# A hybrid decoder layer in split fp32r: gaps of 64 or 32 bytes behind the rows of the transposed activations

## The chip, the cores and the metric

The kernel runs on one core of one Trainium2 chip. The metric is the device time of one execution in microseconds. Three executions of the kernel before took 1139.84, 1139.86 and 1139.87 us, median 1139.86 us.

## The reference, cut to what matters

One layer of a decoder trunk over 256 tokens of width 2048, float32 throughout. The parts that bear on this case are five matrix products and what stands between them:

```python
hn = rmsnorm(x, norm_mix_g)                       # x: 256 x 2048
p = hn @ w_in + b_in                              # 2048 x 6152: conv a/g, q, k, v, o, gates
u = silu(group_norm(causal_dwconv(a * sigmoid(g))))   # 31 taps, 1024 channels
hm = group_norm(mlstm(q, k, v, i, f)) * sigmoid(o)    # 4 heads of 256
x = x + concat([u, hm]) @ w_out                   # 2048 x 2048
up = rmsnorm(x, norm_ffn_g) @ w_up                # 2048 x 11264
h = silu(causal_dwconv(up[:, :5632])) * up[:, 5632:]  # 3 taps
x = x + h @ w_down                                # 5632 x 2048
return rmsnorm(x, norm_final_g)
```

## The kernel before, in words

**Split products.** Each float32 operand is held as two float32r parts, `hi` (the value rounded) and `lo` (value minus `hi`). A product is three matmuls into one PSUM bank: `hi*hi`, `hi*lo` and `lo*hi`. The transposed activations are split once and stay in SBUF: `xp` (16 rows of k, for each row 256 tokens of `hi` and then 256 of `lo`), later `x1p` of the same form in the same place, `mixh` and `mixl` (16 rows of 256), and `ah` and `al` (44 rows of 256, each a buffer of its own). A "row" here is one block of 128 values of k, which lie on the partitions; along a partition a row of `xp` has 2048 bytes and one of `ah` 1024.

**Slabs.** The weights stream through SBUF in slabs, mostly of two rows of k by 512 columns. For each slab SyncE issues the load into one of 5 `raw` buffers, ScalarE casts it into one of 4 `hi` buffers (line 214), VectorE, or GpSimd for some slabs, subtracts into one of 4 `lo` buffers (line 215), and TensorE multiplies. Splitting runs three slabs ahead (`AHEAD`). The order of the work is the order of the slabs list; all other work is hung on slab numbers by `after`.

**Which operand moves.** TensorE loads 128 x 128 weights and streams a moving operand past them; each matmul here has a weight load of its own.

- `ws` groups (lines 241 to 243: conv a/g, q, k): slab columns are loaded as weights, 256 tokens of `xp` stream.
- gate and up (`wp_group`, lines 267 and 268): slab columns are loaded; one row of `x1p`, 512 wide (`hi` and `lo` side by side), streams past the slab's `hi`, then its first 256 past the slab's `lo`.
- `xs` groups (lines 286 to 288: o 344 wide, v and w_out 512 wide, w_down 512 wide) and `down_narrow` (lines 839 to 841, 256 wide): the other way round; 128 tokens of the activations are loaded and the slab's columns stream.

**Where the buffers lie.** In a partition, as the built program places them, taken mod 512 bytes: `xp` and `x1p` begin at 192, `mixh` and `mixl` at 192, `ah` and `al` at 160, all `hi` and `lo` buffers at 160. Every row, every block of 128 columns and every buffer is a multiple of 512 bytes long, so these places hold for every row; the one exception is o, whose 344-wide second row of a slab begins 1376 bytes on, at 0 mod 512. "Lead" below is the place of a weight load minus that of the stream it is loaded beside, mod 512: -32 in `ws`, gate and up; 0 in down and `down_narrow`; +32 in v, w_out and the first rows of o; +192 in the second rows of o.

Of the kernel before, what the change touches and what calls it, by code (L numbers as in the profile page):

```python
# [9 lines left out]
F32 = mybir.dt.float32  # L10
F32R = mybir.dt.float32r
# [4 lines left out]
P = 128  # L16
T = 256
NT = T // P
D = 2048
NK = D // P  # L20
# [4 lines left out]
NF = DFF // P  # L25
# [16 lines left out]
def hybrid_layer_kernel(  # L42
# [11 lines left out]
    cst = ctx.enter_context(tc.tile_pool(name="cst", bufs=1))  # L54
# [7 lines left out]
    def mm_bank(name):  # L62
        return ps.tile([P, 512], F32, tag="mm", name=name, bufs=4)

    def cv_bank(k, name):
        return ps.tile([P, 512], F32, tag=f"cv{k}", name=name)

    def ax_bank(name):
        return ps.tile([P, 512], F32, tag="ax", name=name, bufs=2)
# [7 lines left out]
    def v2(t):  # L77
        return t.rearrange("p (a b) -> p a b", a=2)
# [88 lines left out]
    def after(delay, fn, cost=0.0):  # L167
        tasks[cur[0] + delay].append((fn, cost))
# [48 lines left out]
    def w_slab(wap, kt, nk, col, w, fn, on_pool):  # L217
        if col is None:
            src = wap(kt)
        else:  # L220
            src = wap[kt * P:(kt + nk) * P, col:col + w].rearrange("(k p) c -> p k c", p=P)
        slabs.append(dict(src=src, w=w, nk=nk, mm=fn, pool=on_pool))
# [54 lines left out]
    def xs_slab(wap, col, w, stat, kt, first, last, st, done, on_pool):  # L277
        def fn(hi, lo):
            if first:
                st["b"] = [cv_bank(0, "xs0"), cv_bank(1, "xs1")] if st.get("cv") else [mm_bank("xs0"), mm_bank("xs1")]  # L280
            sh, sl = stat()
            for k in range(2):
                for tt in range(NT):
                    o = st["b"][tt][:, :w]
                    ts_ = slice(tt * P, (tt + 1) * P)
                    pe.matmul(o, sh[:, kt + k, ts_], hi[:, k, :w], start=first and k == 0, stop=False)  # L286
                    pe.matmul(o, sh[:, kt + k, ts_], lo[:, k, :w], start=False, stop=False)  # L287
                    pe.matmul(o, sl[:, kt + k, ts_], hi[:, k, :w], start=False, stop=last and k == 1)  # L288
            if last:
                done(st["b"])  # L290
        w_slab(wap, kt, 2, col, w, fn, on_pool)

    def xs_group(wap, col, w, stat, nk, done, on_pool):
        st = {}
        for kt in range(0, nk, 2):
            xs_slab(wap, col, w, stat, kt, kt == 0, kt + 2 == nk, st, done, on_pool)


    xT = {}
# [318 lines left out]
    def done_out(n):  # L618
        def fn(banks):
            cs = slice(n * 512, (n + 1) * 512)  # L620
            st = {}

            def ev():
                if "h2" not in xT:
                    xT["p2"] = cst.tile([P, NK, 2, T], F32R, tag="xp", name="x1p")
                    xT["h2"], xT["l2"] = xT["p2"][:, :, 0, :], xT["p2"][:, :, 1, :]
                x1 = xres["t"]
                for tt in range(NT):
                    dve.tensor_add(x1[:, tt, cs], x1[:, tt, cs], banks[tt])

            def sq():
                for tt in range(NT):
                    act.activation(banks[tt], xres["t"][:, tt, cs], AF.Square, accum_out=ssq[:, tt, n:n + 1])

            def tr(half):
                def f():
                    b = ax_bank("x1T")
                    st[half] = b
                    for k in range(2):
                        kt = 4 * n + 2 * half + k  # L640
                        for tt in range(NT):
                            pe.transpose(b[:, k * T + tt * P:k * T + (tt + 1) * P], xres["t"][:, tt, kt * P:(kt + 1) * P], ident)
                    for k in range(2):
                        kt = 4 * n + 2 * half + k
                        act.activation(xT["h2"][:, kt, :], v2(b)[:, k, :], AF.Copy, scale=g_ffn[:, kt:kt + 1])
                    for k in range(2):
                        kt = 4 * n + 2 * half + k
                        dve.scalar_tensor_tensor(xT["l2"][:, kt, :], v2(b)[:, k, :], g_ffn[:, kt:kt + 1],
                                                 xT["h2"][:, kt, :].bitcast(F32), op0=ALU.mult, op1=ALU.subtract)
                return f  # L650
            after(1, ev, 1300)
            after(2, tr(0), 800)
            after(3, tr(1), 800)
            after(3, sq)
            if n == 3:
                after(4, rs_ffn)
        return fn

    ffn = {}
# [13 lines left out]
    def open_ffn():  # L673
        if "ah" in ffn:
            return
        inner.close()
        fp = ctx.enter_context(tc.tile_pool(name="ffn", bufs=1))
        ffn["pool"] = fp
        ffn["ah"] = fp.tile([P, NF, T], F32R, tag="ah", name="ah")
        ffn["al"] = fp.tile([P, NF, T], F32R, tag="al", name="al")  # L680
        ffn["gp"] = [fp.tile([P, 2, FK - 1 + T], F32, tag=f"gp{i}", name=f"gp{i}") for i in range(2)]
        for g in ffn["gp"]:
            pool.memset(g[:, :, 0:FK - 1], 0.0)
# [16 lines left out]
    def done_gate(j):  # L700
        def fn(banks):
            s = [None, None]

            def ev():
                open_ffn()
                copy_halves(banks)
# [72 lines left out]
        dve.tensor_mul(o, o, ffn["gf"][:, c0:c0 + w])  # L779

    def load_gf():
        gfb = cst.tile([P, NK, 2, T], F32, tag="xp", name="gfb")
        ffn["gf"] = gfb.rearrange("p a h b -> p (a h b)")[:, 0:D]
        act.dma_start(ffn["gf"], bass.AP(tensor=norm_final_g.tensor, offset=norm_final_g.offset, ap=[[0, P], [1, D]]))

    def done_down(n, c0, w):
        def fn(banks):
            def ev():
                if n == 0:
                    load_gf()  # L790
                for tt in range(NT):
                    add_down(banks[tt], tt, n, c0, w)

            def gmul():
                for tt in range(NT):
                    mul_gf(tt, c0, w)
            after(1, ev)
            after(3, gmul)
            if n == 3:
                after(3, pre_sum)  # L800
        return fn
# [67 lines left out]
    for b in range(3):  # L869
        xs_group(w_in, OFF_O + OW * b, OW, get_xT, NK, done_o(b), True)  # L870
# [6 lines left out]
    for hp in range(2):  # L877
        xs_group(w_in, OFF_V + 512 * hp, W, get_xT, NK, done_v(hp), True)
# [17 lines left out]
    for n in range(3):  # L896
        xs_group(w_down, 512 * n, W, lambda: (ffn["ah"], ffn["al"]), NF, done_down(n, 512 * n, W), False)
# [1 line left out]
    down_narrow(4, 1792, 256, 4, SPLIT_BUFS)  # L899


    xT["p"] = cst.tile([P, NK, 2, T], F32R, tag="xp", name="xp")
    xT["h"], xT["l"] = xT["p"][:, :, 0, :], xT["p"][:, :, 1, :]
    for c in range(NK // 2):
        sl = slice(c * T, (c + 1) * T)
        if c:
# [73 lines left out]
    for i in range(len(slabs)):  # L980
# [30 lines left out]
        while bg and credit > 0:  # L1011
            name = bg[0][0].__name__
# [40 lines left out]
```

## Time and profile before

| | |
|---|---|
| median of three executions | 1139.86 us |
| the profiled execution, its own time | 1139.86 us |
| its span in the trace | 1138.1 us |
| granted TensorE clock, mean over the span | 0.998 |
| PE busy, matmuls | 1125.4 us, 6756 |
| weight loads busy | 1007.7 us |
| VectorE, ScalarE, GpSimd busy | 746.4, 579.4, 131.3 us |
| DMA | 215.43 MB, 189 GB/s |

The busy time of PE counts each matmul from its start to a modelled end, and neighbours overlap. What a matmul costs in a stream is therefore read here from starts: the distance between the starts of two neighbours. In the timeline the columns are the start, the duration (both us), the engine, the line, the operation, out<-in, the array's part and the stream's shape.

### The profile page before, as it was taken

How to read it: one execution, taken by the hardware profiler on the slowest of the kernel's cores; microseconds unless marked ns; L12 is line 12 of the kernel's file. 1: busy time of each engine (PE TensorE's matmuls, PEld its weight loads, DVE VectorE, ACT ScalarE, POOL GpSimd, SP SyncE). 2: the span in 40 equal slices, each digit the busy share in tenths (PEclk: the TensorE clock that was granted, in tenths of full speed). 3: DMA queues.
4: the chain of work that ended last, by engine and by line, in shares of the span. 5: the costliest groups of instructions: out<-in, count | busy, mean ns of one | idle time of the engine just before them, and what ended most of it. 6: DMA issues, size and time to landing. Idle time of an engine off the chain costs nothing.

```text
span 1138.1 us, 17456 instructions
## 1 busy us (share of the span) xinstructions
PE 1125.4 (99%) x6756; PEld 1007.7 (89%) x6756; DVE 746.4 (66%) x1138; ACT 579.4 (51%) x824; POOL 131.3 (12%) x100
## 2 busy tenths in 40 slices
PE   8999999999999999999999999999999999999997
PEld 8999999998888888888888888888888888888997
DVE  5498999987656457667666666676576645454543
ACT  4744576754445455545555555455555434343432
POOL 0343554534300000000000000000000000000000
PEclk9999999999999999999999999999999999999999
DMA  8864565565655666666666666666666667656652
GB/s 269 250 187 123 183 220 169 178 195 168 204 193 171 189 184 182 191 192 194 184 190 192 183 196 188 193 190 188 188 184 193 195 197 228 196 190 196 192 186 76
DMA packets 128459, 215.43 MB, mean 189 GB/s; under 512 B 7456, under 2 KB 44920, under 8 KB 127864
## 3 DMA queue, kind: packets, MB, share of 16 engines
q1 hardware_dynamic: 126824, 209.99, 60.9%
q10 hardware_dynamic: 1552, 4.33, 1.0%
q8 instruction: 53, 0.87, 0.3%
q14 instruction: 30, 0.25, 0.1%
HBM read 212.19 MB, written 2.10 MB: 188 GB/s over the span
## 4 chain that ended last, share of the span: by engine, by line
PE 95%; DVE 3%; ACT 1%; issue 1%; POOL 0%; POOLq 0%; ACTq 0%
PE gate L267 14%; PE up L267 14%; PE xs L287 9%; PE xs L286 9%; PE xs L288 9%; PE up L268 7%; PE gate L268 7%; PE ws L243 5%; PE ws L241 5%; PE ws L242 5%; PE xs L841 2%; PE xs L840 2%; PE xs L839 2%; DVE conv L376 2%; DVE lo L215 1%
## 5 line engine op out<-in xcount | busy, mean ns | idle before, releaser
L215 DVE TENSOR_TENSOR lo<-raw,hi 128x1024 fp32r<-128x1024 f32 (+2 forms) x353 | 435.2, 1234 | 327.3 <-ACT hi L214 321.3
L214 ACT CAST hi<-raw 128x1024 fp32r<-128x1024 f32 (+2 forms) x400 | 411.7, 1032 | 452.8 <-PE xs L288 153.4
L267 PE MATMUL gate<-x1p,hi 128*128 128x512 f32 x704 | 245.0, 390 | 0.0
L267 PE MATMUL up<-x1p,hi 128*128 128x512 f32 x704 | 244.5, 390 | 0.0
L268 PE MATMUL up<-x1p,lo 128*128 128x256 f32 x704 | 198.5, 282 | 0.0
L268 PE MATMUL gate<-x1p,lo 128*128 128x256 f32 x704 | 198.5, 282 | 0.0
L267 PEld LDWEIGHTS up<-x1p,hi 128*128 128x128 f32 x704 | 132.2, 188 | 27.7
L267 PEld LDWEIGHTS gate<-x1p,hi 128*128 128x128 f32 x704 | 132.2, 188 | 27.6
L241 PE MATMUL ws<-xp,hi 128*128 128x256 f32 x512 | 145.2, 284 | 1.8 <-ACT hi L214 1.8
L243 PE MATMUL ws<-xp,lo 128*128 128x256 f32 x512 | 143.2, 280 | 1.5 <-DVE lo L215 1.5
L242 PE MATMUL ws<-xp,hi 128*128 128x256 f32 x512 | 143.0, 279 | 0.0
L268 PEld LDWEIGHTS gate<-x1p,lo 128*128 128x128 f32 x704 | 133.1, 189 | 0.0
L268 PEld LDWEIGHTS up<-x1p,lo 128*128 128x128 f32 x704 | 133.1, 189 | 0.0
L215 POOL TENSOR_TENSOR lo<-raw,hi 128x1024 fp32r<-128x1024 f32 (+1 forms) x48 | 110.6, 2308 | 152.3 <-ACT hi L214 114.3
L287 PE MATMUL xs<-lo,ah 128*128 128x512 f32 x264 | 102.7, 389 | 0.0
L288 PE MATMUL xs<-hi,al 128*128 128x512 f32 x264 | 102.7, 389 | 0.0
L286 PE MATMUL xs<-hi,ah 128*128 128x512 f32 x264 | 102.7, 389 | 0.0
L241 PEld LDWEIGHTS ws<-xp,hi 128*128 128x128 f32 x512 | 96.4, 188 | 3.0 <-ACT hi L214 2.3
L243 PEld LDWEIGHTS ws<-xp,lo 128*128 128x128 f32 x512 | 96.2, 188 | 2.4 <-DVE lo L215 2.1
L376 DVE SCALAR_TENSOR_TENSOR conv<-up,cB,conv 128x256 f32<-128x256 f32 x240 | 97.6, 478 | 0.0
L242 PEld LDWEIGHTS ws<-xp,hi 128*128 128x128 f32 x512 | 96.3, 188 | 0.0
L815 POOL TENSOR_TENSOR rf<-ms,halves 128x1 f32<-128x1 f32 x2 | 1.1, 552 | 714.9 <-DVE ms L813 714.9
(184 smaller groups left out, 1399.0 us busy)
## 6 DMA issues: line engine op xcount, KB each, us to landing
raw<-in_w_up_dram SPq DMA_DIRECT2D x176, 512.0 KB, 4.0
raw<-in_w_down_dram SPq DMA_DIRECT2D x88, 512.0 KB, 4.6
raw<-in_w_in_dram SPq DMA_DIRECT2D x48, 512.0 KB, 4.0
raw<-in_w_in_dram SPq DMA_DIRECT2D x64, 256.0 KB, 4.6
raw<-in_w_out_dram SPq DMA_DIRECT2D x32, 512.0 KB, 4.4
raw<-in_w_in_dram SPq DMA_DIRECT2D x24, 344.0 KB, 3.3
x<-in_x_dram ACTq DMA_DIRECT2D x2, 1024.0 KB, 7.5
xs<-in_x_dram SPq DMA_DIRECT2D x7, 256.0 KB, 5.6
```

What stands on the lines that cost most here:

```text
L214: act.copy(hi[:, c], raw[:, c])
L215: s["eng"].tensor_sub(lo[:, c], raw[:, c], hi[:, c].bitcast(F32))
L241: pe.matmul(o, hi[:, k, cs], mh[:, kt + k, :], start=first, stop=False, skip_group_check=True)
L242: pe.matmul(o, hi[:, k, cs], ml[:, kt + k, :], start=False, stop=False, skip_group_check=True)
L243: pe.matmul(o, lo[:, k, cs], mh[:, kt + k, :], start=False, stop=last, skip_group_check=True)
L267: pe.matmul(o, hi[:, k, cs], m2, start=first, stop=last, skip_group_check=True)
L268: pe.matmul(o[:, 0:T], lo[:, k, cs], mp[:, kt + k, 0, :], start=False, stop=last, skip_group_check=True)
L286: pe.matmul(o, sh[:, kt + k, ts_], hi[:, k, :w], start=first and k == 0, stop=False)
L287: pe.matmul(o, sh[:, kt + k, ts_], lo[:, k, :w], start=False, stop=False)
L288: pe.matmul(o, sl[:, kt + k, ts_], hi[:, k, :w], start=False, stop=last and k == 1)
L376: dve.scalar_tensor_tensor(a, up[c][:, t:t + T], cB[:, 8 * t + c:8 * t + c + 1], a, op0=ALU.mult, op1=ALU.add)
L839: pe.matmul(o, sh[:, kt, ts_], hi[:, k, :], start=kt == 0, stop=False)
```

## The change

The rows of `xp` and `x1p` get 16 unused words (64 bytes) behind every two rows, and those of `ah` and `al` 8 words (32 bytes) behind every four. A small class maps a row's number to its place; the whole buffer is rounded up to a multiple of 512 bytes (33280 bytes in place of 32768, 45568 in place of 45056), so that all other buffers keep their places mod 512. `mixh` and `mixl` stay as they were. The final gain vector, which shares the buffer of `xp`, gets a buffer of the new size.

No instruction is added, removed or moved: on all five engines the instructions stand in the same order, with the same shapes and the same waits; only addresses differ. A slab number p counts from 0 to 7 within a group over `xp`, and g = 0 to 10 counts the fours of rows of `ah`. After the change `xp`'s rows lie at 192 + 64 p mod 512, and `ah`'s at 160 + 32 g.

```diff
+    class Rows:
+        def __init__(self, pool_, tag, name, n, shape, run, gap):
+            self.n, self.shape, self.run, self.gap, self.part = n, shape, run, gap, None
...
+            words = n * self.size + (n // run - 1) * gap
+            self.t = pool_.tile([P, (words + 127) // 128 * 128], F32R, tag=tag, name=name)
...
+        def __getitem__(self, key):
+            k, rest = key[1], key[2:]
+            one = isinstance(k, int)
+            k0, k1 = (k, k + 1) if one else (k.start, k.stop)
+            assert k0 // self.run == (k1 - 1) // self.run
+            o = k0 // self.run * self.gap
+            v = self.t[:, o + k0 * self.size:o + k1 * self.size]
...
+    def x_rows(name):
+        r = Rows(cst, "xp", name, NK, (2, T), 2, 16)
+        return r, r.half(0), r.half(1)
...
-                    xT["p2"] = cst.tile([P, NK, 2, T], F32R, tag="xp", name="x1p")
-                    xT["h2"], xT["l2"] = xT["p2"][:, :, 0, :], xT["p2"][:, :, 1, :]
+                    xT["p2"], xT["h2"], xT["l2"] = x_rows("x1p")
...
-        ffn["ah"] = fp.tile([P, NF, T], F32R, tag="ah", name="ah")
-        ffn["al"] = fp.tile([P, NF, T], F32R, tag="al", name="al")
+        for n in ("ah", "al"):
+            ffn[n] = Rows(fp, n, n, NF, (T,), 4, 8)
...
-        gfb = cst.tile([P, NK, 2, T], F32, tag="xp", name="gfb")
-        ffn["gf"] = gfb.rearrange("p a h b -> p (a h b)")[:, 0:D]
+        gfb = cst.tile([P, NK * 2 * T + 128], F32, tag="xp", name="gfb")
+        ffn["gf"] = gfb[:, 0:D]
...
-    xT["p"] = cst.tile([P, NK, 2, T], F32R, tag="xp", name="xp")
-    xT["h"], xT["l"] = xT["p"][:, :, 0, :], xT["p"][:, :, 1, :]
+    xT["p"], xT["h"], xT["l"] = x_rows("xp")
```

## Rows read from the trace of the kernel before

**Rows 1.** The page: busy time by engine, and the granted TensorE clock in 40 slices.
```profile
PE 1125.4 (99%) x6756; PEld 1007.7 (89%) x6756; DVE 746.4 (66%) x1138; ACT 579.4 (51%) x824; POOL 131.3 (12%) x100
PEclk9999999999999999999999999999999999999999
```

**Rows 2.** Waits of TensorE: its line, releaser, us in total, times, longest.
```profile
PE ws L241 <- ACT hi L214: 1.8, 2, 1.1
PE ws L243 <- DVE lo L215: 1.5, 3, 0.8
```

**Rows 3.** Matmul groups by form: count | busy us, mean ns of one | idle before.
```profile
L267 PE MATMUL gate<-x1p,hi 128*128 128x512 f32 x704 | 245.0, 390 | 0.0
...
L241 PE MATMUL ws<-xp,hi 128*128 128x256 f32 x512 | 145.2, 284 | 1.8 <-ACT hi L214 1.8
...
L286 PE MATMUL xs<-hi,ah 128*128 128x512 f32 x264 | 102.7, 389 | 0.0
...
L839 PE MATMUL xs<-hi,ah 128*128 128x256 f32 x176 | 49.8, 283 | 0.0
...
L286 PE MATMUL xs<-hi,xp 128*128 128x344 f32 x96 | 30.8, 321 | 0.0
...
L286 PE MATMUL xs<-hi,xp 128*128 128x512 f32 x64 | 25.9, 405 | 0.0
```

**Rows 4.** Timeline of PE in gate, first and last of 51 matmuls.
```profile
499.79 0.28 PE L268 MATMUL gate<-x1p,lo 128*128 128x256 f32 x1
...
508.45 0.28 PE L268 MATMUL gate<-x1p,lo 128*128 128x256 f32 x1
```

**Rows 5.** Timeline of PE in `ws`, first and last of 62 matmuls.
```profile
69.81 0.28 PE L243 MATMUL ws<-xp,lo 128*128 128x256 f32 x1
...
76.99 0.28 PE L241 MATMUL ws<-xp,hi 128*128 128x256 f32 x1
```

**Rows 6.** Timeline of PE in down, first and last of 50 matmuls.
```profile
949.82 0.39 PE L288 MATMUL xs<-hi,al 128*128 128x512 f32 x1
...
960.93 0.39 PE L286 MATMUL xs<-hi,ah 128*128 128x512 f32 x1
```

**Rows 7.** Timeline of PE in `down_narrow`, first and last of 56 matmuls.
```profile
1089.80 0.28 PE L840 MATMUL xs<-lo,ah 128*128 128x256 f32 x1
...
1096.40 0.28 PE L841 MATMUL xs<-hi,al 128*128 128x256 f32 x1
```

**Rows 8.** Timeline of PE in v, first and last of 53 matmuls.
```profile
254.66 0.40 PE L288 MATMUL xs<-hi,xp 128*128 128x512 f32 x1
...
266.79 0.40 PE L286 MATMUL xs<-hi,xp 128*128 128x512 f32 x1
```

**Rows 9.** Timeline of PE in o: a slab's first row, its second, the next slab.
```profile
131.50 0.32 PE L286 MATMUL xs<-hi,xp 128*128 128x344 f32 x1
...
132.44 0.32 PE L286 MATMUL xs<-hi,xp 128*128 128x344 f32 x1
...
133.38 0.32 PE L286 MATMUL xs<-hi,xp 128*128 128x344 f32 x1
```

**Rows 10.** Timeline of PE at the fp32 scores between two slabs.
```profile
245.28 1.02 PE L560 MATMUL S<-qkt 128*128 128x256 f32 x4
246.14 0.61 PE L562 MATMUL S<-qkt 128*128 128x128 f32 x4
```

**Rows 11.** Weight loads (PEld) and matmuls beside each other in `down_narrow`.
```profile
1126.04 0.28 PE L839 MATMUL xs<-hi,ah 128*128 128x256 f32 x1
1126.05 0.19 PEld L840 LDWEIGHTS xs<-lo,ah 128*128 128x128 f32 x1
```

**Rows 12.** Stretches: length, busy us (count) of each engine, granted clock, DMA share, GB/s.
```profile
100.00:200.00 100.00, 99.09 (x741) 97.61 (x740) 93.89 (x198) 61.48 (x86) 48.34 (x25) 1.00 0.59 182
...
600.00:700.00 100.00, 100.00 (x579) 88.67 (x578) 69.19 (x96) 54.40 (x81) 0.00 (x0) 1.00 0.65 189
...
1000.00:1140.00 140.00, 130.52 (x825) 118.78 (x823) 63.97 (x68) 52.43 (x64) 1.10 (x2) 0.98 0.52 166
```

More of the change, by code (lines that the diff above doesn't have):

```diff
@@ L296, in xs_group, with half @@
             xs_slab(wap, col, w, stat, kt, kt == 0, kt + 2 == nk, st, done, on_pool)
+    class Rows:
+        def __init__(self, pool_, tag, name, n, shape, run, gap):
+            self.n, self.shape, self.run, self.gap, self.part = n, shape, run, gap, None
+            self.size = 1
+            for d in shape:
+                self.size *= d
+            words = n * self.size + (n // run - 1) * gap
+            self.t = pool_.tile([P, (words + 127) // 128 * 128], F32R, tag=tag, name=name)
+        def half(self, part):
+            r = object.__new__(Rows)
+            r.__dict__.update(self.__dict__, part=part)
+            return r
+        def __getitem__(self, key):
[5 more added lines that the diff above has]
+            v = self.t[:, o + k0 * self.size:o + k1 * self.size]
+            if len(self.shape) == 2:
+                v = v.rearrange("p (k h t) -> p k h t", k=k1 - k0, h=self.shape[0])
+            else:
+                v = v.rearrange("p (k t) -> p k t", k=k1 - k0)
+            if self.part is not None:
+                rest = (self.part,) + rest
+            return v[(slice(None), 0 if one else slice(None)) + rest]
+    def x_rows(name):
+        r = Rows(cst, "xp", name, NK, (2, T), 2, 16)
+        return r, r.half(0), r.half(1)
     xT = {}
```

## The prediction, made blind

> **What bounds the kernel now.** I read the page's busy times first: TensorE is busy 99% of the span, at the granted clock of 2.4 GHz in every slice [rows 1]. Then its waits: it stood still for the split operands only a few times, 1.8 and 1.5 us in the two largest sums [rows 2]. So the time is TensorE's own stream, and the question is what one matmul of that stream costs. The groups by form give the counts [rows 3]; their mean durations overlap and are of no use for a cost. So I went to the timeline and divided the distance of two starts by the matmuls between them. At 2.4 GHz, n columns take n/2.4 ns; what is left over I call the excess.
>
> - gate and up: 25 pairs of a 512 and a 256 in 8.66 us, 346.4 ns a pair; 768 columns are 320.0; excess 26.4 a pair [rows 4].
> - `ws`: 61 steps in 7.18 us, 117.7 ns against 106.7; excess 11.0 [rows 5].
> - down: 49 steps in 11.11 us, 226.7 against 213.3; excess 13.4 [rows 6].
> - `down_narrow`: 55 steps in 6.60 us, 120.0 against 106.7; excess 13.3 [rows 7].
> - v: 52 steps in 12.13 us, 233.3 against 213.3; excess 20.0 [rows 8].
> - o: 12 steps in 1.88 us, 156.7 against 143.3; excess 13.4 [rows 9].
> - the fp32 scores, which use none of the changed places: 4 steps in 0.86 us, 215 ns; taken as two times 256 columns (213.3), an excess of 1.7 [rows 10].
>
> The counts are three lines to a group, two for the gate/up lines [rows 3]: gate and up 2 x 704 = 1408 pairs, `ws` 1536, down 792, narrow 528, v 192, o 288. Times the excess: 37.2 + 16.9 + 10.6 + 7.0 + 3.8 + 3.9 = 79.4 us. That is all the change can act on. w_out has an excess too, but its activations are not touched.
>
> Why an address could matter: the weight load of the next matmul starts 0.01 us after the current matmul [rows 11], so at each start two reads of SBUF begin together, one at the stream's place and one at the load's. Down and v run the same shape in the same way and differ in their buffers' places alone: lead 0 costs 226.7 [rows 6], lead +32 costs 233.3 [rows 8]. The clock is at 2.4 GHz in both. So 32 bytes go with 6.6 ns, unless something else in those stages does it.
>
> **The change part by part.** Nothing is added or moved in the instruction streams, so the sum has only one kind of term: matmuls whose lead changes, times the change of the excess.
>
> How many change: over `xp` and `x1p`, p = 0 keeps its place and 7 of 8 slabs move, by 64 to 448 bytes. Over `ah` and `al`, g = 0 keeps its place (4 of 44 rows) and 40 of 44 move, by 32 to 320 bytes.
>
> The price at the new leads the trace mostly does not show; it has leads -32, 0, +32 and, in the second rows of o, +192. I bound it from both sides.
>
> Lower end: all moved matmuls fall to the excess of the fp32 scores, 1.7 (3.4 a pair). Gate and up 1408 x 23.0 x 7/8 = 28.3; `ws` 1536 x 9.3 x 7/8 = 12.5; down 792 x 11.7 x 40/44 = 8.4; narrow 528 x 11.6 x 40/44 = 5.6; v 192 x 18.3 x 7/8 = 3.1; o 288 x 11.7 x 7/8 = 2.9. Sum 60.8 us gained, 1079 us.
>
> Upper end: all moved matmuls rise to the excess of v, 20.0 (40 a pair). Gate and up 1408 x 13.6 x 7/8 = 16.8; `ws` 1536 x 9.0 x 7/8 = 12.1; down 792 x 6.6 x 40/44 = 4.8; narrow 528 x 6.7 x 40/44 = 3.2; o 288 x 6.6 x 7/8 = 1.7. Sum 38.6 us lost, 1178 us.
>
> Between them one row speaks directly: in o, the first row of each slab has lead +32 and the second +192, and both take 0.94 us for six matmuls [rows 9]. A lead of 192 there does not bring the excess down. That argues against the lower end, for one width and one place. Against it stands the step between down and v. I take the reading that the present leads, all within 32 bytes of zero but for that half of o, are the bad neighbourhood for part of the places only, and count a quarter of the lower end's gain: 15.2 us. The quarter is a choice: zero is what o says, one is what the scores say, and o has the same kind of operands.
>
> Of this, o's quarter, 0.7 us, I leave out. In the stretch that holds o VectorE is busy for 93.9 of 100 us [rows 12]; a faster TensorE there would wait for the split and for the convolution's taps. In gate/up VectorE has 69.2 and the DMA engines 65% [rows 12], so a shorter pair is collected in full. Sum 14.5 us. The profiled execution took 1139.86 us, the median of the three as well: 1139.86 - 14.5 = 1125.4 us.
>
> The 512 bytes by which later buffers shift, and the gain vector's new shape, cost nothing: same instructions, same places mod 512. That places 512 bytes apart are alike is borne out by down: a slab's matmuls there load from four places 512 or 1024 bytes apart, and down and narrow, with streams 2048 and 1024 bytes long, have the same excess [rows 6, 7].
>
> [...] The rows show an excess over the columns' time in every split stage and almost none in the scores [rows 4 to 8, 10]. [...]
>
> **The rivals.**
>
> 1. The lead does not matter; the excess belongs to changing the weights in fp32r. For: o's equal halves [rows 9]; the excess is much the same at 512 and 256 columns in down, 13.4 and 13.3 [rows 6, 7]. Against: down and v. Then no term of the sum is left, and the time is 1139.9 us, within 0.2% (1137.6 to 1142.1; that is about what a measurement of this kernel can tell from no change). Chance 0.24. [...]
>
> 2. Slower: what counts is the place within 64 bytes. Loads at a multiple of 64 against streams 32 bytes off it are v's case (192 and 160); loads and streams both 32 off are down's (160 and 160). The steps of 64 in `xp` change nothing then. The steps of 32 in `ah` turn every odd g into v's case: 5 of 11 fours, 20 of 44 rows. Down: 792 x 20/44 = 360 matmuls x 6.6 ns = 2.4 us. Narrow: 240 x up to 6.6 = 1.6 us, its price at that place not being shown. 1142.3 to 1143.9 us. For: down against v is just this pair of places. Against: o's second row begins at a multiple of 64 and its first does not, and they cost the same. It decides if odd fours of down stand at 233 and even ones at 227. A wider form, where most new leads cost what v's does, goes up to the upper end. Chance 0.29 together: 0.19 for the narrow form, 0.10 for the wider.
>
> 3. TensorE gets faster and the work around it becomes the bound. VectorE's 93.9 of 100 us in the early stretch [rows 12] allow at most 6% there, while in the stretches after it the engines have a third free. The early stages hold v, o and `ws`: with a quarter of their gain lost wholly, 15.2 falls to 15.2 - (12.5 + 3.1 + 2.9)/4 = 10.6 us, 1129.3 us. It is part of the forecast's own range.
>
> **How the numbers follow.** The forecast, that spreading the leads takes away part of the excess, has 0.47: 1125.4 us, its own range from half of the lower end (30.4 us, 1109.5) to 1137. Of it 0.46 is faster by over 0.2% and 0.01 within. No effect of the lead: 0.24, within. Slower: 0.29. So faster 0.46, same 0.25, slower 0.29. For eight in ten I leave out about one in ten on each side: below, the case that well over half of the removable excess goes; above, the wide form of the slower rival. That gives 1104 to 1147 us.
>
> **What would show it.** The steps of gate and up by slab number p: the forecast wants p = 0 near 346 ns a pair and several others clearly below; in down g = 0 near 227 and others below. w_out must stay at its step of before. Rival 1 would show all steps as they are now; rival 2 odd fours at 233 and nothing in gate and up. The forecast is wrong if no slab's step falls, or if rises over some slabs eat the falls over others.

## The result and the profile after

The changed kernel takes 1149.82 us (median of 4, 1148.92 to 1150.53) against 1139.86 us: ratio 1.0085, 95% interval 1.0073 to 1.0097. It is slower by 0.85%, 10 us, where 14.5 us of gain had been forecast, and it lies above the stated range.

The page of the changed kernel: busy times by engine and the granted clock, to be laid beside [rows 1].

```profile
PE 1136.7 (99%) x6756; PEld 1009.2 (88%) x6756; DVE 742.9 (65%) x1138; ACT 579.2 (50%) x824; POOL 131.5 (11%) x100
PEclk9999999999999999999999999999999999999999
```

TensorE's waits in the changed kernel, the answer to [rows 2]:

```profile
PE ws L241 <- ACT hi L214: 1.8, 2, 1.1
PE ws L243 <- DVE lo L215: 1.1, 3, 0.8
```

So the same 6756 matmuls run without more waiting and take 11 us more. The 40 slices of the page are too coarse for one stretch, from 16 to 20 us. Its row in the kernel before and in the changed one (length, busy us and count of TensorE, granted clock, DMA share, GB/s):

```profile
16.00:20.00 4.00, 4.00 (x37) 1.00 0.93 290
...
16.00:20.00 4.00, 4.00 (x23) 0.57 0.99 305
```

There the granted clock of this profiled execution was 0.57 of full speed on the mean, and 0.50 from 17 to 19 us, against 1.00 in the kernel before. Twelve `ws` steps took 213 ns each in place of about 120, some 1.1 us in all. In the 2 us ahead of the stretch TensorE was busy for 1.24 us at a granted clock of 1.00 in both kernels, and only in one of them the clock fell; why, no run here shows. The two longer of the four executions (1150.53 and 1150.46 us) have a mean clock of 0.997 over the span, the two shorter ones (1149.18 and 1148.92 us) one of 0.999 and 0.998, and the median lies between them.

The rest of the time lies in the steps of the stream. The timeline of TensorE in the changed kernel, first matmuls only: two in w_out, 48 steps apart; those of the gate slabs p = 0 to 4 (8 pairs each); those of the fours g = 0, 1, 2 and 6 to 9 of down (24 matmuls each); two in narrow, 24 apart.

```profile
371.83 0.40 PE L286 MATMUL xs<-hi,mixh 128*128 128x512 f32 x1
...
383.03 0.40 PE L286 MATMUL xs<-hi,mixh 128*128 128x512 f32 x1
...
626.04 0.39 PE L267 MATMUL gate<-x1p,hi 128*128 128x512 f32 x1
...
628.81 0.39 PE L267 MATMUL gate<-x1p,hi 128*128 128x512 f32 x1
...
631.65 0.39 PE L267 MATMUL gate<-x1p,hi 128*128 128x512 f32 x1
...
634.42 0.39 PE L267 MATMUL gate<-x1p,hi 128*128 128x512 f32 x1
...
637.24 0.39 PE L267 MATMUL gate<-x1p,hi 128*128 128x512 f32 x1
...
956.05 0.39 PE L286 MATMUL xs<-hi,ah 128*128 128x512 f32 x1
...
961.53 0.39 PE L286 MATMUL xs<-hi,ah 128*128 128x512 f32 x1
...
967.12 0.40 PE L286 MATMUL xs<-hi,ah 128*128 128x512 f32 x1
...
989.53 0.40 PE L286 MATMUL xs<-hi,ah 128*128 128x512 f32 x1
...
995.04 0.40 PE L286 MATMUL xs<-hi,ah 128*128 128x512 f32 x1
...
1000.63 0.39 PE L286 MATMUL xs<-hi,ah 128*128 128x512 f32 x1
...
1006.08 0.39 PE L286 MATMUL xs<-hi,ah 128*128 128x512 f32 x1
...
1084.20 0.28 PE L872 MATMUL xs<-hi,ah 128*128 128x256 f32 x1
...
1087.03 0.28 PE L872 MATMUL xs<-hi,ah 128*128 128x256 f32 x1
```

- Gate: 2.77, 2.84, 2.77 and 2.82 us a slab, 346, 355, 346 and 352 ns a pair. The medians over all 22 groups are 347.2, 354.4, 347.0 and 351.6, and p = 4 to 7 repeat them: the pattern returns after four steps of 64 bytes. Before it was 346.4 [rows 4].
- Down: 5.48 us at g = 0 (228 a matmul), 5.59 at g = 1 (233), 5.51 at g = 6 (230), 5.59 at g = 7, and at g = 8, 256 bytes on, 5.45 us: 227, the step of before [rows 6]. The other fours stand at 233 to 234.
- Narrow: 2.83 us for 24, 117.9, cheaper than before's 120.0 [rows 7].
- w_out, untouched: 11.20 us for 48, 233.3, what v has [rows 8].

The steps of each stage added up over the whole trace, in us:

| | before | after | difference |
|---|---|---|---|
| `ws` | 184.8 | 187.2 | +2.4 |
| o, v | 91.2 | 91.3 | +0.2 |
| w_out | 90.4 | 90.4 | 0.0 |
| gate and up | 488.4 | 493.1 | +4.7 |
| down | 179.5 | 183.7 | +4.1 |
| narrow | 63.2 | 62.4 | -0.8 |

That is 10.5 of the 10.7 us between the profiled executions (1139.86 and 1150.53). Some 1.1 of the 2.4 us in `ws` belong to the stretch from 16 to 20 us; that leaves 9.4 us for the leads.

### The profile page after: what moved, and what is told of

Same layout as the page of the kernel before. It is cut to its first block, busy times and chain, and to the rows that moved or that the text cites. A ratio compares the mean times of both kernels' runs of the same rounds, so it can differ in the third digit from the quotient of the medians.

```text
span 1148.8 us, 17456 instructions
## 1 busy us (share of the span) xinstructions
PE 1136.7 (99%) x6756; PEld 1009.2 (88%) x6756; DVE 742.9 (65%) x1138; ACT 579.2 (50%) x824; POOL 131.5 (11%) x100
## 4 chain that ended last, share of the span: by engine, by line
PE 96%; DVE 1%; ACT 1%; issue 1%; POOL 0%; POOLq 0%; ACTq 0%
PE gate L267 14%; PE up L267 14%; PE xs L287 10%; PE xs L288 10%; PE xs L286 10%; PE up L268 7%; PE gate L268 7%; PE ws L243 5%; PE ws L241 5%; PE ws L242 5%; PE xs L874 2%; PE xs L872 2%; PE xs L873 2%; DVE conv L410 1%; DVE lo L215 0%
```

## The experiments

After the result the theory was L: what a matmul costs here is set by the lead mod 256 bytes. Its rivals were J (not the lead but its change costs), N (a cause outside the leads), A (the places themselves, not their difference).

The edits of e1 to e4, e7, e8 and e10 are shown against the changed kernel, those of e5, e6, e9, e11 and e12 against the kernel before; `...` stands for lines left out.

**One half of the change each: e1_xp_only and e2_ah_only.**

```diff
-            ffn[n] = Rows(fp, n, n, NF, (T,), 4, 8)     # e1
+            ffn[n] = Rows(fp, n, n, NF, (T,), 4, 0)
...
-        r = Rows(cst, "xp", name, NK, (2, T), 2, 16)    # e2
+        r = Rows(cst, "xp", name, NK, (2, T), 2, 0)
...
```

> The 64-byte gaps in xp alone; ah and al as before. Theory L (what a matmul costs depends on its lead, the place of the weight load minus that of the stream, mod 256 bytes): the stages over xp cost what they cost in the changed kernel, gate and up 354.4 a pair in slabs p = 1 and 5, 351.5 in p = 3 and 7, 347 in the others, and down is back at 226.7; sum of gate/up and the ws groups +7 us, 1147 us. Theory J (not the lead costs but its change from slab to slab, after which the stream has to settle again): the same here. Rival theory N (the gain and the loss come from elsewhere, such as later buffers shifted by 512 bytes): both stages slower, near 1150, or neither.

> The 32-byte gaps in ah and al alone; xp as before. L and J: gate and up stay at 346.7 a pair, down costs what it does in the changed kernel (about 227 at g = 0 and 8, 229.4 at g = 6, 233 at the others), narrow falls to about 118; +4.1 - 0.8 = +3.3 us, 1143.2 us. N: no difference from before, or the whole of the loss.

e1 took 1145.63 us, ratio 1.0049 (1.0032 to 1.0065); gate and up had 173.6 to 177.2 a matmul by the same slabs as in the changed kernel, and down 226.7. e2 took 1143.25 us, 1.0027 (1.0018 to 1.0037); down stood at 233 but for g = 0, 6 and 8, gate and up at 346.7 a pair. 5.8 and 3.4 us make 9.1 of the 10 us, close to the 9.4 that the leads have without the stretch from 16 to 20 us. N falls. e1's `ws` steps were up by 1.1 us, and its trace has no such stretch; the changed kernel's 2.4 less some 1.1 come to about the same.

**The period: e3_gaps_256.**

```diff
+        r = Rows(cst, "xp", name, NK, (2, T), 4, 64)
...
+            ffn[n] = Rows(fp, n, n, NF, (T,), 22, 64)
...
```

> Gaps of 256 bytes: behind every four rows of xp, and one behind the first 22 rows of ah and al. The lead changes from slab to slab, but by 256 bytes only. L: mod 256 nothing changes, 1139.9 us within 1, gate and up 346.7 a pair everywhere, down 226.7. A lead mod 512: rows at +256 cost otherwise, 2 us or more either way. J: the first matmuls behind each change settle anew, as the 256 + 132 pair in p = 1 of the changed kernel does; three changes a group, +1.5 to +3 us.

1139.87 us, ratio 0.9999 (0.9989 to 1.0008). Timeline of TensorE in this kernel: 40 pairs of gate, 240 matmuls of down, changes of 256 bytes among them.

```profile
621.25 0.39 PE L267 MATMUL gate<-x1p,hi 128*128 128x512 f32 x1
...
635.12 0.39 PE L267 MATMUL gate<-x1p,hi 128*128 128x512 f32 x1
...
947.35 0.39 PE L286 MATMUL xs<-hi,ah 128*128 128x512 f32 x1
...
1001.75 0.39 PE L286 MATMUL xs<-hi,ah 128*128 128x512 f32 x1
```

13.87 us by 40 is 346.8, 54.40 by 240 is 226.7: nothing happens. In this kernel the gaps as such cost nothing, later buffers pushed on by 1024 bytes cost nothing, and places 256 bytes apart are alike.

**A constant lead of +32: e4_ah_plus32.**

```diff
...
+        r = Rows(cst, "xp", name, NK, (2, T), 2, 0)
...
+            ffn[n] = Rows(fp, n, n, NF, (T,), 4, 0, 8)     # eight words ahead of row 0, no gaps
...
```

> ah and al begin 32 bytes later, no gaps: lead +32 in all of down and narrow, constant. L: down 233.4 a matmul everywhere, as v and w_out have it, 792 x 6.7 = +5.3 us; narrow about 118, 528 x 2 = -1.0 us; 1144.1 us. J: the lead is constant, so the stream settles once: 226.7 and 1139.9 us.

1144.24 us, 1.0036 (1.0023 to 1.0049): 4.4 us, where L said 4.2. Three starts in down, 24 matmuls apart:

```profile
949.04 0.40 PE L286 MATMUL xs<-hi,ah 128*128 128x512 f32 x1
...
954.64 0.40 PE L286 MATMUL xs<-hi,ah 128*128 128x512 f32 x1
...
960.24 0.40 PE L286 MATMUL xs<-hi,ah 128*128 128x512 f32 x1
```

5.60 us for 24, 233.3 each, with no change of lead anywhere: 32 bytes of lead are worth 6.6 ns on every matmul of 512 columns in down. Narrow went the other way, to 118.3. J as the whole cause falls.

**All places moved, all leads kept: e5_all_plus32.**

```diff
+    cst.tile([P, 8], F32, tag="pad", name="pad")
     ident = cst.tile([P, P], F32, tag="ident", name="ident")
```

> The kernel before with an unused block of 32 bytes ahead of the first buffer: every buffer lies 32 bytes later, every lead is as before. L (the difference of the two places counts): no stage changes, 1139.9 us within 0.5. Rival A (the places themselves count, such as whether a load or a stream begins at a multiple of 64): streams over xp now begin 32 off, loads from the slabs at a multiple of 64, so gate/up, ws and down change, 2 us or more either way.

1139.84 us, 0.9998 (0.9989 to 1.0007). Two starts in down, 240 matmuls apart (the line numbers are one higher here):

```profile
947.32 0.39 PE L287 MATMUL xs<-hi,ah 128*128 128x512 f32 x1
...
1001.72 0.39 PE L287 MATMUL xs<-hi,ah 128*128 128x512 f32 x1
```

54.40 by 240 is 226.7; gate and up 346.6 a pair, w_out 233.3, all as before. A falls for this shift: with the difference kept, 32 bytes more on both sides change nothing.

**w_out from lead +32 to 0: e6_mix_160.**

```diff
+    mid.tile([P, 120], F32, tag="pad0", name="pad0")
     mixh = mid.tile([P, NK, T], F32R, tag="mixh", name="mixh")
     mixl = mid.tile([P, NK, T], F32R, tag="mixl", name="mixl")
+    mid.tile([P, 8], F32, tag="pad1", name="pad1")
```

> The kernel before with mixh and mixl moved by -32 mod 512 (480 unused bytes ahead of them, 32 behind): lead 0 in w_out in place of +32, all else at its place. L: w_out falls from 233.4 to 226.7 a matmul, 384 x 6.7 = -2.6 us, 1137.3 us. If w_out's price has another reason than its lead: 1139.9 us.

1137.72 us, 0.9980 (0.9971 to 0.9989): 2.1 us less, where L said 2.6. Two starts in w_out, 48 steps apart:

```profile
367.70 0.39 PE L286 MATMUL xs<-hi,mixh 128*128 128x512 f32 x1
...
378.58 0.39 PE L286 MATMUL xs<-hi,mixh 128*128 128x512 f32 x1
```

10.88 us, 226.7, against 11.20 us in the changed kernel's rows above. What e4 took from down, e6 gives back to w_out.

**The lead against its change: e7_xp_plus64.**

```diff
...
+        r = Rows(cst, "xp", name, NK, (2, T), 2, 0, 16)    # 64 bytes ahead of row 0, no gaps
...
+            ffn[n] = Rows(fp, n, n, NF, (T,), 4, 0)
```

> xp begins 64 bytes later, no gaps: gate, up and ws have the lead of p = 1 of the changed kernel, -96, throughout. Tells the price of that lead from the price of changing to it: if the 256 + 132 pair of each such slab is the change's, gate and up stand at 349 to 350 a pair (1408 x 3 = +4 us), and at 354.4 (+10.9 us) if it belongs to the lead. ws by p = 1's price +2 a matmul, +3 us. 1147 us by the one, 1154 us by the other.

1148.03 us, 1.0072 (1.0058 to 1.0086). Gate in this kernel, first matmuls of three slabs:

```profile
627.12 0.39 PE L267 MATMUL gate<-x1p,hi 128*128 128x512 f32 x1
...
629.92 0.39 PE L267 MATMUL gate<-x1p,hi 128*128 128x512 f32 x1
...
632.72 0.39 PE L267 MATMUL gate<-x1p,hi 128*128 128x512 f32 x1
```

2.80 us a slab, 350.0 a pair: the lead -96 costs 3.3 a pair when it stays. In the changed kernel the same lead is entered anew in p = 1, and this is that slab's third pair between its neighbours:

```profile
629.16 0.39 PE L267 MATMUL gate<-x1p,hi 128*128 128x512 f32 x1
629.39 0.28 PE L268 MATMUL gate<-x1p,lo 128*128 128x256 f32 x1
629.51 0.42 PE L267 MATMUL gate<-x1p,hi 128*128 128x512 f32 x1
629.76 0.30 PE L268 MATMUL gate<-x1p,lo 128*128 128x256 f32 x1
629.90 0.39 PE L267 MATMUL gate<-x1p,hi 128*128 128x512 f32 x1
```

From 629.51 to 629.90 it takes 0.39 us in place of 0.35. So J was right in part: of the 7.7 ns a pair that p = 1 and 5 cost, 3.3 belong to the lead and 4.4, some 35 ns a slab, to changing to it. `ws` stood at 120.0 in every slab that no other work broke up; in the changed kernel its p = 1 has 119.9, so there the change costs nothing.

**A scan over the leads: e8_scan_32_16 and e10_scan_16.**

```diff
+        r = Rows(cst, "xp", name, NK, (2, T), 2, 8)        # e8: leads of ws -32 to -256
...
+            ffn[n] = Rows(fp, n, n, NF, (T,), 2, 4)        #     leads of down 0 to 336
...
+        r = Rows(cst, "xp", name, NK, (2, T), 2, 4, 32)    # e10: leads of ws -160 to -272
...
+            ffn[n] = Rows(fp, n, n, NF, (T,), 4, 0)        #      no gaps in ah and al
```

> A look over the leads: xp with 32 bytes behind every two rows (leads -32 to -256 over the eight slabs), ah and al with 16 bytes behind every two rows (leads 0 to 336 over 22 slabs). L: the leads that other runs have come out as there (-96: 349 to 354 a pair, -160: 347, -224: 351.5; in down 0, 256 and -32: 227 to 229, +32 and most others 233), and -256, the lead of 0, as good as any. Places 16 bytes apart have no row yet; if the price goes by 32-byte lines they stand like a neighbour. About 1146 to 1150 us.

> A look at 16-byte steps: xp begins 128 bytes later and has 16 bytes behind every two rows, leads -160 to -272 over the eight slabs. If the price of a lead goes by 32-byte lines, -176 and -208 stand like a neighbour and ws is lowest, near 114, in one or two slabs around -192; else a lower one can appear between.

e8 took 1149.14 us, 1.0079 (1.0065 to 1.0093). Its `ws` slab at lead -192, 24 matmuls, and its v slab at lead 0, 11 steps:

```profile
168.97 0.28 PE L241 MATMUL ws<-xp,hi 128*128 128x256 f32 x1
...
171.70 0.28 PE L241 MATMUL ws<-xp,hi 128*128 128x256 f32 x1
...
271.79 0.39 PE L286 MATMUL xs<-hi,xp 128*128 128x512 f32 x1
...
274.28 0.40 PE L288 MATMUL xs<-hi,xp 128*128 128x512 f32 x1
```

2.73 us by 24 is 113.8, the lowest `ws` step of the runs up to here; 2.49 by 11 is 226.4, so v too is cheap at 0. In down the steps were 227.0 at 0, 227.4 at 16, 232.6 at 32, 233.3 at 224, 228.3 at 240, 226.7 at 256, 227.3 at 272: a valley of about 16 bytes to either side, not a line of 32. The expected 227 to 229 at -32, which is 224 mod 256, did not come; a second, shallower dip lies at 176 and 192 instead, with 229.6 and 229.2. Expected had been that lead 0 would serve gate and up as well: the slab at -256 had 353.5 a pair, entered by a change; a constant lead 0 was not tried there. e10, one execution, 1144.04 us: `ws` 118.8, 118.7, 114.5, 119.2, 118.3, 117.2, 119.7 and 119.1 in its undisturbed group; only -192 is low, and -176 and -208 do not stand like it.

**Leads chosen: e9_leads_chosen and e11_xp_plus160.**

```diff
+    def xp_at(name, o):
+        t = cst.tile([P, NK * 2 * T + 128], F32R, tag="xp", name=name)
+        return t[:, o:o + NK * 2 * T].rearrange("p (k h t) -> p k h t", k=NK, h=2)
...
+                    xT["p2"] = xp_at("x1p", 0)
...
-    xT["p"] = cst.tile([P, NK, 2, T], F32R, tag="xp", name="xp")
+    xT["p"] = xp_at("xp", 40)      # e9 has e6's two pads as well
...
```

> No gaps; constant leads, chosen from the looks so far: xp begins 160 bytes later (ws at lead -192, v and o at +192), x1p stays (gate and up at -32), mixh and mixl at lead 0 as in the earlier run. L: ws 113.8 a matmul in place of 117.7 (1536 x 3.9 = -6.0 us), o +1.4 (288 x 1.4 = +0.4), v unchanged at 233, w_out -2.1; 1139.9 - 7.7 = 1132.2 us, a little more where the early stretch waits for VectorE. If the 113.8 of that one slab was a step that only a change of lead gives: ws at 117 or above, 1138 us.

> The same shift of xp alone, mixh and mixl as before. L: 1134.3 us. With the run beside it, it tells whether the two gains add up.

e9 took 1133.06 us, 0.9940 (0.9928 to 0.9953); e11 1135.18, 0.9959 (0.9945 to 0.9972); 1132.2 and 1134.3 had been expected. The two gains add up (2.1 and 4.7 us), and e9 beats both kernels. v, which was expected unchanged at 233, came down at its constant lead of +192; two starts in e9, 72 matmuls apart:

```profile
249.41 0.39 PE L286 MATMUL xs<-hi,xp 128*128 128x512 f32 x1
...
265.89 0.39 PE L286 MATMUL xs<-hi,xp 128*128 128x512 f32 x1
```

16.48 by 72 is 228.9: a third price at 512 columns, and it stands where down had its second dip. `ws` gained 4.1 us, not 6.0, because part of its groups stayed at 117.8. Two stretches of e11's timeline at the same lead, 144 `ws` matmuls of conv a/g and 96 of q:

```profile
62.41 0.28 PE L241 MATMUL ws<-xp,hi 128*128 128x256 f32 x1
...
79.37 0.28 PE L241 MATMUL ws<-xp,hi 128*128 128x256 f32 x1
...
157.98 0.28 PE L241 MATMUL ws<-xp,hi 128*128 128x256 f32 x1
...
168.86 0.28 PE L241 MATMUL ws<-xp,hi 128*128 128x256 f32 x1
```

16.96 by 144 is 117.8, 10.88 by 96 is 113.3.

**Two patterns at one lead: e12_kick.**

```diff
...
+            o = (32 if k < 2 else 40) + (2 * k + self.half) * T     # rows 0 and 1 32 bytes lower
+            return self.t[:, o:o + T][:, key[2]]
...
```

> The chosen constant leads, but the first two rows of xp lie 32 bytes lower: each ws group begins with one slab at lead -160 and runs the other seven at -192. In the kernel with -192 throughout, the conv a/g groups 1 to 3 stay at 117.8 a matmul and the q and k groups at 113.3. Theory E (a lead has more than one settled pattern, and how the stream enters decides which): after the change of lead conv a/g settles at 113.6 as in the look over the leads, 21 slabs x 24 x 4.2 = -2.1 us, the first slabs of q and k lose 0.4; 1131.4 us. If the pattern belongs to what else runs in the conv a/g groups: no gain, 1133.1 to 1133.5 us.

1134.65 us, 0.9955 (0.9942 to 0.9969): slower than e9, so the gain did not come. Yet the last conv a/g group ran at 113.3 in five of its slabs, and the first q group, 113.3 in e9, at 117.8. The pattern does not belong to the group: one lead has two settled patterns. In e9 it changes within a group, behind a break in which TensorE transposes something else; starts of `ws` slabs, 48 matmuls apart ahead of the break and behind it:

```profile
36.01 0.28 PE L241 MATMUL ws<-xp,hi 128*128 128x256 f32 x1
...
41.45 0.28 PE L241 MATMUL ws<-xp,hi 128*128 128x256 f32 x1
...
50.80 0.32 PE L149 MATMUL tr<-ident,rows_D 88*128 88x88 f32 x2
...
53.81 0.28 PE L241 MATMUL ws<-xp,hi 128*128 128x256 f32 x1
...
59.47 0.28 PE L241 MATMUL ws<-xp,hi 128*128 128x256 f32 x1
```

5.44 by 48 is 113.3 before it, 5.66 by 48 is 117.9 behind it. Two breaks just ahead of it, at 44.2 us (transposes too) and 47.6 us, changed nothing, and e12's change of lead did not steer it as hoped: what picks the pattern is open. It may make executions of one kernel differ: in e2 one took 1141.77 us and the others 1142.78 to 1143.54, and the one of 1141.77, which was profiled, had its `ws` slabs at 116.7 where before has many at 117.8, with `xp` in its old place (`ws` 1.3 us shorter in all). The others have no trace, so that this is the whole of the difference is not shown.

## Why the prediction was wrong

- What bounds the kernel was right: the waits are as before, the clock too but for the stretch from 16 to 20 us (0.57 of full speed), and the loss is in the stream's steps. Of the 2.4 GHz and the n/2.4 ns from which the excess is counted, the rows show the slope: at lead 0 a step of 512 columns takes 226.7 - 120.0 = 106.7 ns more than one of 256 [rows 6, 7], which is 2.4 columns a ns. The traces give the clock as a share of full speed only.
- That the lead matters was right. e4 moved only the loads' place and e6 only that of w_out, and 226.7 and 233.3 changed places. Rival 1 falls. The runs show how long a step is, not what makes it longer.
- The step that failed: "I take the reading that the present leads, all within 32 bytes of zero but for that half of o, are the bad neighbourhood for part of the places only, and count a quarter of the lower end's gain". In down and in gate and up the leads of before are among the cheap ones: 0 in down is the bottom of a valley (227.0 against 232.6 at 32 in e8), and -32 in gate and up, at 346.7 a pair, is 3.3 better than -96 at 350.0 (e7). The lower end, of which the quarter was taken, came from the scores' excess of 1.7, an estimate that takes their step of 215 ns as two times 256 columns [rows 10]; no split stage of any run came near it (the lowest are 6.6 in `ws`, at 113.3, and about 13 at 512 columns, at 226.7). By terms (forecast by that quarter, then measured): gate and up -7.1, +4.7; `ws` -3.1, +2.4 (about 1.3 without the stretch from 16 to 20 us); down -2.1, +4.1; narrow -1.4, -0.8; v -0.8, 0.0. Only narrow has the forecast's sign.
- Down against v was in the prediction and was read for one thing only, that the lead matters. It also says in which direction: away from 0, down gets dearer by 6.6. The upper end's term from it, 4.8 us, is close to the 4.1 measured. Taking each stage's new price from the nearest row of the same shape would have given the sign for down.
- The o row was read too broadly: two equal prices were taken for no dependence. In before a row of o has 156.3 at +32 and 156.0 at +192, and these two happen to cost the same. At +96 it has 159.2 (first rows in e7) and 159.0 (second rows in e9), at 256 it has 157.5 (second rows in e7). A slab of e9, its first row at +192, its second at 352, which is +96 mod 256, and the next slab:

```profile
121.23 0.31 PE L286 MATMUL xs<-hi,xp 128*128 128x344 f32 x1
...
122.16 0.32 PE L286 MATMUL xs<-hi,xp 128*128 128x344 f32 x1
...
123.11 0.31 PE L286 MATMUL xs<-hi,xp 128*128 128x344 f32 x1
```

0.93 and 0.95 us for six, where before had 0.94 and 0.94 [rows 9].

- Rival 2 named the right sign and the wrong rule. In its narrow form even fours of down and all of gate and up would not move; they do, g = 2 and 4 at 233. Its wide form held for down (32 of 44 rows at about v's price) and not for gate and up, 4.7 of 16.8 us. With 0.10 for the wide form the range ended at 1147, 2.8 us short.
- Missing from the sum was the price of changing a lead, about 35 ns for a slab of p = 1 or 5 of gate and up (e7); for the 44 such slabs that makes about 1.5 of their 4.7 us.
- The costs set at nothing, the shift of the later buffers and the gain vector's new shape, were nothing (e3, and e5 for another shift). That VectorE would bind a faster early stretch was not borne out: e9's `ws` got faster by 4.1 us.

## What to carry to other kernels

Where TensorE's stream is the bound and every matmul has its own weight load, read the steps of equal matmuls in different stages: if they differ, compare where the loaded and the streamed buffers begin, and try a constant offset for each stage. Spreading the offsets bought here the average over cheap and dear ones, and at some of the changes a price of its own: 10 us more, where the constant offsets of e9 took 6.8 us off. A row that shows that something matters also shows in which direction; use it for both.

## What the runs showed of the hardware that had not been expected

- A 512-column fp32r matmul in these streams takes from 226.7 to 233.3 ns by the lead alone: 226.7 at 0 (down, e6), 228.9 at +192 (e9), 233.3 at +32 (e4). The price returns after 256 bytes (226.7 in down and 346.8 a pair in gate with changes of 256, e3), and there is a valley of some 16 bytes to either side of 0 (227.0 at 0, 227.4 at 16 and 228.3 at 240, but 232.6 at 32 and 233.3 at 224, e8). A shift of everything by 32 bytes does not count (226.7 in down, 1139.84 us in all, e5). Why, no run here shows.
- The cheap lead differs from stage to stage: 0 is good at 512 columns (226.7 in down and w_out, 226.4 in v in e8) and, where it stays, dear at 256 in narrow (120.0 against 118.3 at +32, e4); the lowest steps of `ws` stand at -192 (113.3, e9 and e11).
- One lead can have two settled patterns, 113.3 and 117.8 in `ws` at -192, that last for many slabs, whole groups among them. They changed at a break in the stream (113.3 to 117.9, e9) and at a change of lead (e12), but not at every one; what picks one of them is open.
